# When p is turned and split in the last stage of an encoder layer, and when embedding weights may take raw slots

## The chip, the cores and the metric

One core of a Trainium2 chip runs the whole kernel. The metric is device microseconds of one launch, as a median over runs; lower is better.

## The reference, cut to what matters

N = 2048 tokens of width D = 1024 pass one encoder layer. What this change touches is the per-layer embedding, which the last layer norm takes in:

```python
x = layernorm(ALPHA * x0 + mix, ln1_g, ln1_b)              # x1 in the kernel
ffn = hierarchical_moe(x, ...)                             # two of 32 experts for each token
ple = sigmoid(x @ w_ple_gate + b_ple_gate) * (p @ w_ple_proj)   # 1024x1024 and 256x1024
out = layernorm(ALPHA * x + ffn + ple, ln2_g, ln2_b)
```

All products have to be of float32 accuracy.

## The kernel before, in words

A float32 product is made of three products of fp32r parts: every operand is split into a high part `hi` (a copy on ScalarE) and a low part `lo` (source minus `hi`, on VectorE). `split` (lines 304 and 305) does both, and `mm3` (lines 219 to 221) issues the three matmuls `hi*hi`, `hi*lo`, `lo*hi`. 128 tokens are a tile; there are 16.

**Places.** Buffers are slots of 4 KB per partition, handed out oldest-freed first. `SF` (tile `FB`, later also the region `FY`) holds split operands: 26 slots, and 12 more of `FY` during the mixer. `SR` (`RB`) holds raw rows and weights: 9 slots, and 12 more (`RY`) once `FY` has been given up. `SP` is the eight PSUM banks of 128x512; a pair of banks is two neighbours that begin at an even number, and of the free pairs the one whose later-freed bank has been free longest is taken. A taker that finds nothing free lets the other jobs go on until there is something. On the chip a buffer's next writer waits for its last reader.

**Order.** The program's text fixes which buffers every instruction gets. Running work (`run`) lets background jobs (`Background`, `start`, `need`) make a step after each `mm3`. A planner then orders the instructions of each engine by the times that it estimates, and each engine works through its own list in that order.

**Stages.** Mixer; output projection (`wo_tiles`), router and routing; the region passes from split to raw slots ("the region changes hands"); the embedding of tiles 10 to 15 (`PRE`, function `embed`); the 32 experts; the last stage.

**Weights.** From the last group of `wo_tiles` on, `load_weights` brings raw weights (line 1036, queue of SyncE) in the order: embedding for tiles 10 and 11, embedding for 12 to 15, experts, embedding for the last stage. It takes a raw slot only while more than `rkeep + rclaims` are free; `rkeep` is 3 and becomes 4 before the last stage. `split_weights` turns a raw weight into two split slots when two are free beyond `claims`. After the region's hand-over come `bp`, the broadcast bias of the gate (line 1296, issued by GpSimd), and the rows of p and x1 of tiles 10 and 11.

**Last stage.** For tiles 0 to 9 (`END`) one after the other, `embed_tile` takes a pair of banks, runs 48 matmuls for the gate (16 `mm3`), gives the tile's two slots of x1 back, adds the bias on VectorE (line 1231, once for each half of the columns), takes tanh on ScalarE (line 1232), runs 12 matmuls for the product with p, and combines (lines 1236, 1245). The 20 slots of embedding weights stay in place. `load_x1` brings x1's high and low parts of a tile, already split, into two slots (line 1145). `load_p` does the same for p of a pair of tiles: raw rows (line 1092), four transposes on TensorE into one bank (line 1125), one split slot, `split` with 512 columns each, and only then is the bank free:

```python
        b = SP.get()
        for k in range(4):
            nc.tensor.transpose(PS[:, b, k * 128:(k + 1) * 128], RB[:, r, k * 128:(k + 1) * 128], ident)
        SR.free(r)
        yield
        q, = yield from claimed(1)
        split(FB[:, q, :512], FB[:, q, 512:], PS[:, b])
        SP.free(b)
```

`release_p` frees p's slot after the second tile of its pair. `prepare_tile(i)` starts these jobs: for tile 0 while the last expert ends, for tile 1 just ahead of the loop, and for tile i + 2 after tile i. Called p0, p2, p4, p6, p8 are the p of tiles 0 and 1, 2 and 3, and so on.

Behind this runs `finish` for every tile: the gathered rows of the two experts (line 1616, GpSimd) are added with their weights (line 1653, VectorE), then mean, variance and the norm on GpSimd (1659, 1663 to 1665), ScalarE (1661, 1667), VectorE (1668) and VectorE or GpSimd (1669), and the output is stored (1672, issued by ScalarE).

Of the kernel before, what the change touches and what calls it, by code (L numbers as in the profile page):

```python
# [16 lines left out]
N = 2048  # L17
# [11 lines left out]
# Rows that the r-th fullest expert has a fixed place for; what goes beyond runs in a loop.  # L29
# [9 lines left out]
def most_further_blocks():  # L39
    """At least the most blocks beyond the fixed ones: counts fall with the rank, each is at most N, 2 N in all."""  # L40
    best = 0
    for m in range(1, NE + 1):
        need = [0] * m
        for r in range(m - 1, -1, -1):
            need[r] = max(CAPS[r] + 1, need[r + 1] if r + 1 < m else 0)
        left = 2 * N - sum(need)
        if left >= 0 and need[0] <= N:
            best = max(best, sum(-(-(need[r] - CAPS[r]) // 128) for r in range(m)) + left // 128 + m)
    return best
# [3 lines left out]
# first tiles, whose normalised rows are computed a second time for the residual  # L53
AGAIN = 8
# tiles at the end that take the rows of their experts before their embedding
# [3 lines left out]
def interleave(a, b):  # L59
    """The items of b spread evenly between those of a."""  # L60
    out = []
    for i, v in enumerate(a):
        out.append(v)
        out += b[i * len(b) // len(a):(i + 1) * len(b) // len(a)]
    return out
# [5 lines left out]
# tiles whose embedding comes before the experts, and after them  # L71
PRE, END = ([10, 11], [12, 13, 14, 15]), [0, 1, 2, 3, 4, 5, 6, 7, 8, 9]


class Slots:
    """A region cut into equal slots; the slot that has been free longest goes first."""

    def __init__(self, *parts):
        self.runs, n = [], 0
        for m in parts:  # L80
            self.runs.append((n, m))
            n += m
        self.age = {i: i - n for i in range(n)}
        self.clock = 0
        # slots from here on are only for those that ask for any; they take them first
        self.limit = 999
# [37 lines left out]
class Parts:  # L124
    """Slots of several tiles under one numbering."""
# [17 lines left out]
class Background:  # L143
    """Work that prepares what the tensor engine needs next, spread over the steps of the running work."""
# [36 lines left out]
def hybrid_conv_pool_hmoe_encoder(ctx, tc, x, p, ln0_g, ln0_b, w_in, b_in, conv_w, pool_w, pool_scale,  # L181
# [9 lines left out]
    # a region of the split tiles' at first, of the plain ones' later  # L191
# [34 lines left out]
    # constants  # L226
# [9 lines left out]
    # loads the table of functions while the first rows are on their way  # L236
# [34 lines left out]
    def start(name, gen, rate):  # L271
        jobs[name] = gen
        bg.add(gen, rate)

    def need(name):
        """Ends a job; the others go on when it has to wait for them."""
        if name in jobs:
            gen = jobs.pop(name)
            n = 0
            while next(gen, DONE) is not DONE:  # L280
                n += 1
                if n > 40:
                    bg.step()
            bg.forget(gen)

    # layer norm of a row tile in place
# [27 lines left out]
    # ---------------------------------------------------------------- mixer, first half  # L314
# [9 lines left out]
    def prep(c):  # L324
# [8 lines left out]
        for q in range(2):  # L333
# [15 lines left out]
            # gain and shift come after the transposes, where they are scalars of the partitions  # L349
# [31 lines left out]
    def again():  # L381
        """The rows of the first tiles, for which nothing is kept while the tensor engine waits for them."""
        gr0.append(SR.get())
        gr0.append(SR.get())
        nc.scalar.dma_start(RB[:, gr0[0]], bcast(ln0_g, D))
        nc.scalar.dma_start(RB[:, gr0[1]], bcast(ln0_b, D))
        for t in range(AGAIN):
            yield from wait(SR, keep=2)
            r = SR.get()
            nc.sync.dma_start(RB[:, r], xf[t * 128:(t + 1) * 128, :])  # L390
            yield
            v = RB[:, r]
            s = ln_stats(v)
            yield
            ln_apply(v, s, RB[:, gr0[0]], RB[:, gr0[1]])
            nc.gpsimd.dma_start(x0d[t * 128:(t + 1) * 128, :], v)
            SR.free(r)
            yield
# [21 lines left out]
    def load_w(s, j):  # L420
        """The four channel tiles h, gate_c, gate_b, u of group j."""
        for i in range(4):
            if (s, j, i) not in raw:
                yield from wait(SR)
                fetch_w(s, j, i)
                yield
            yield from wait(SF)
            hi = SF.get()
            yield from wait(SF)
            lo = SF.get()  # L430
            r = raw.pop((s, j, i))
            split(FB[:, hi], FB[:, lo], RB[:, r])
            SR.free(r)
            wz[s, j, i] = (hi, lo)
            yield
# [105 lines left out]
    # per-channel constants as columns: b_in, conv_w, pool_scale, ln0_g, ln0_b  # L541
# [9 lines left out]
    b = SP.get()  # L551
# [20 lines left out]
    def load_wo():  # L572
        """The output projection; its rows for the pools come times the pools' own products and scales."""
# [86 lines left out]
    # ---------------------------------------------------------------- mixer, second half; router  # L660
# [12 lines left out]
    # high parts next to low parts, and high parts alone  # L673
# [39 lines left out]
    def post(t, b, skip):  # L713
        """Residual, layer norm, x1 to memory and, transposed and split, to the chunk's tiles."""
# [70 lines left out]
    # ---------------------------------------------------------------- routing  # L785
# [33 lines left out]
    # by the rank of an expert: first row and rows of its whole blocks, rows of all its fixed places,  # L819
    # what a row's number beyond the whole blocks changes by, and the same beyond the fixed places  # L820
# [8 lines left out]
    def first_max(dst, val, best, n):  # L829
        """One-hot of the first place along the last axis where val equals best."""  # L830
# [5 lines left out]
    def expm(dst, tmp):  # L836
        """exp of values that are at most 0, from tanh of their halves."""
# [47 lines left out]
    def table(dst, val):  # L885
        """val[rank] by its slopes, ranks along the partitions."""
# [16 lines left out]
    def dispatch():  # L903
# [11 lines left out]
        # rank of every expert by its count, the lower number first among equals  # L915
# [21 lines left out]
        # further blocks, and how many come before every expert's  # L937
# [39 lines left out]
        # the token of every place: one-hot of the place in its block times the token's number at its block  # L977
# [30 lines left out]
    # ---------------------------------------------------------------- weights of experts and embedding, in their order  # L1008
# [32 lines left out]
    def split_weights():  # L1041
        while True:
# [6 lines left out]
            if kind == "P" and i % 5 == 4:  # L1049
                # half the product, for the sigmoid as (tanh + 1) / 2  # L1050
# [8 lines left out]
    # slots of the split tiles' that work under way is to get before further weights do  # L1059
    claims, rclaims = [0], [0]  # L1060
    rkeep, routed = [3], []
# [24 lines left out]
    # ---------------------------------------------------------------- per-layer embedding  # L1086
# [27 lines left out]
    def load_p(ts):  # L1114
        """The transposed parts of two tiles' rows of p, high and low halves in one slot."""
# [46 lines left out]
    def embed(ts, lhs, w, done, halves=(0, 1)):  # L1162
        """Gate times product and the residual, a half of the columns after the other."""
# [51 lines left out]
    def embed_tile(t, ws):  # L1215
        """The same for one tile, with all the weights at hand."""
# [36 lines left out]
    # ---------------------------------------------------------------- order of the work from here on  # L1253
# [34 lines left out]
    # the region changes hands  # L1288
# [5 lines left out]
    SR.add(NR, NY)  # L1294
    bp = SR.get()
# [53 lines left out]
    # every block: the tokens of its rows, its first row, whether it is half; the blocks of every expert  # L1349
# [46 lines left out]
    # ---------------------------------------------------------------- experts  # L1396
    def product(o, xs, k, wh, wl, start, stop):
        """Rows times weights. Half blocks hold high and low parts side by side: their products add up later."""
# [7 lines left out]
    def stage1(ns, w):  # L1406
        """Both products of the blocks ns with w1 and w3, every weight tile once."""
# [112 lines left out]
    # ---------------------------------------------------------------- rows beyond the fixed blocks  # L1520
# [48 lines left out]
    # ---------------------------------------------------------------- rows in the fixed blocks  # L1569
# [13 lines left out]
    def prepare_tile(i):  # L1583
        if i < len(END):
            t = END[i]
            if i % 2 == 0:
                claims[0] += 1
                start(f"p{t}", load_p(END[i:i + 2]), 1.0)
            claims[0] += 2
            start(f"x{t}", load_x1(t, True), 1.0)  # L1590

# [11 lines left out]
    # ---------------------------------------------------------------- combination and last layer norm  # L1603
    yq = {}

    def fetch(ts):
        """For every tile the rows of the two experts of its tokens, and what they are added to."""
# [13 lines left out]
    def finish_last(t):  # L1621
        """The rows of the experts before the embedding, which ends the work of the tensor engine."""
# [22 lines left out]
    def finish(t):  # L1645
# [12 lines left out]
        # mean from the sum, variance from the squares about it  # L1658
# [64 lines left out]
```

## Time and profile before

| what | value |
|---|---|
| median of three runs | 1624.23 us (1621.86 to 1624.94) |
| span of the profiled execution | 1625.7 us; no time of its own is given beside the span |
| TensorE busy | 1572.1 us, 97% of the span |
| VectorE, ScalarE, GpSimd busy | 71%, 49%, 29% |
| last matmul ends | 1610.4 us after the span's start |

The profiled execution's span lies 1.5 us above the median. TensorE is busy nearly throughout, so what counts are the few stretches in which it stands still or runs at a lower granted clock.

### The profile page before, as it was taken

What the parts mean: (1) busy time and instruction counts of PE and PEld (TensorE: products, weight loads), DVE (VectorE), ACT (ScalarE), POOL (GpSimd) and SP (SyncE); (2) the same over time, 40 slices, a digit from 0 to 9 for tenths busy, and PEclk for the clock granted to TensorE, in tenths of its full rate; (3) what the DMA queues carried; (4) which work ended last, traced back from release to release, by engine and by line L of the source; (5) the groups of instructions that cost most, each with busy time, mean ns of one, the idle gap of its engine ahead of it and who ended that gap; (6) DMA issues with size and microseconds to landing.
All of it is one profiled execution on the core that took longest, in us unless ns stands there. A gap on an engine that the chain in (4) does not pass through costs nothing.

```text
span 1625.7 us, 21580 instructions
## 1 busy us (share of the span) xinstructions
PE 1572.1 (97%) x7370; PEld 1293.2 (80%) x7371; DVE 1157.1 (71%) x1406; ACT 792.6 (49%) x940; POOL 476.4 (29%) x626
## 2 busy tenths in 40 slices
PE   6999999999999998999999999999999999999986
PEld 6887888887888887778888888888888888888865
DVE  6777484345666767758878788777888767776887
ACT  7343242113111124147777777677777657662332
POOL 3454152443232225010212111111212101006874
PEclk9999999999999999999999999999999999999988
DMA  6547268865375536469898998998898987998871
GB/s 207 183 154 222 65 186 293 299 248 165 116 264 196 178 120 240 141 217 381 310 381 322 359 352 303 355 357 333 324 360 313 347 275 268 369 338 327 325 272 65
DMA packets 204810, 427.88 MB, mean 263 GB/s; under 512 B 18857, under 2 KB 70617, under 8 KB 204697
## 3 DMA queue, kind: packets, MB, share of 16 engines
q1 hardware_dynamic: 162096, 292.33, 51.6%
q0 software_dynamic: 34080, 122.96, 20.4%
q10 hardware_dynamic: 8520, 11.18, 2.1%
q8 instruction: 59, 0.97, 0.2%
q14 instruction: 55, 0.44, 0.1%
HBM read 333.10 MB, written 93.32 MB: 262 GB/s over the span
## 4 chain that ended last, share of the span: by engine, by line
PE 37%; issue 11%; POOL 4%; DVE 1%; DMA 1%; ACT 1%; POOLq 0%; DVEq 0%; ACTq 0%; SPq 0%
PE PS L219 9%; PE PS L221 9%; PE PS L220 9%; PE PS L1403 3%; PE PS L1404 3%; PE PS L311 2%; POOL RY L1616 1%; PE PS L1461 1%; DMA yd<-RB 1%; DVE RB L1653 0%; POOL RY L1669 0%; POOL RB L1616 0%; POOL rstd L1664 0%; PE PS L1331 0%; POOL rstd L1663 0%
## 5 line engine op out<-in xcount | busy, mean ns | idle before, releaser
L220 PE MATMUL PS<-FB 128*128 128x512 f32 (+1 forms) x1516 | 590.2, 389 | 5.5 <-DVE FB L305 5.5
L219 PE MATMUL PS<-FB 128*128 128x512 f32 (+1 forms) x1436 | 560.0, 392 | 12.8 <-DVE FB L305 8.1
L221 PE MATMUL PS<-FB 128*128 128x512 f32 (+1 forms) x1436 | 558.4, 390 | 3.1 <-DVE FB L305 3.1
L220 PEld LDWEIGHTS PS<-FB 128*128 128x128 f32 x1516 | 287.9, 190 | 62.2 <-DVE FB L305 6.2
L219 PEld LDWEIGHTS PS<-FB 128*128 128x128 f32 x1436 | 272.7, 190 | 68.1 <-DVE FB L305 9.0
L221 PEld LDWEIGHTS PS<-FB 128*128 128x128 f32 x1436 | 272.4, 190 | 57.9 <-DVE FB L305 3.5
L305 DVE TENSOR_TENSOR FB<-RY,FB 128x1024 fp32r<-128x1024 f32 x232 | 280.8, 1229 | 52.1 <-ACT FB L304 25.7
L305 DVE TENSOR_TENSOR FB<-RB,FB 128x1024 fp32r<-128x1024 f32 x212 | 257.4, 1227 | 79.6 <-ACT FB L304 67.8
L304 ACT CAST FB<-RB 128x1024 fp32r<-128x1024 f32 x216 | 223.7, 1049 | 148.5 <-PE PS L220 50.1
L304 ACT CAST FB<-RY 128x1024 fp32r<-128x1024 f32 x236 | 243.6, 1051 | 92.9 <-PE PS L220 45.1
L1316 POOL DMA_INDIRECT RY<-x1d,TBI x29 | 56.5, 1948 | 391.8 <-DVE FB L305 217.2
L305 DVE TENSOR_TENSOR FB<-PS,FB 128x1024 fp32r<-128x1024 f32 (+1 forms) x116 | 103.1, 897 | 68.4 <-ACT FB L304 68.2
L304 ACT CAST FB<-PS 128x1024 fp32r<-128x1024 f32 (+1 forms) x116 | 86.4, 759 | 113.7 <-PE PS L311 75.6
L220 PE MATMUL PS<-FB,FY 128*128 128x512 f32 x264 | 104.4, 396 | 0.0
L1403 PE MATMUL PS<-FB 128*128 128x512 f32 x264 | 103.9, 394 | 0.0
L1404 PE MATMUL PS<-FB 128*128 128x512 f32 x264 | 103.2, 391 | 0.0
L219 PE MATMUL PS<-FB,FY 128*128 128x512 f32 x216 | 86.0, 398 | 0.0
L221 PE MATMUL PS<-FB,FY 128*128 128x512 f32 x216 | 85.6, 396 | 0.0
L219 PE MATMUL PS<-FY,FB 128*128 128x512 f32 x180 | 72.1, 400 | 0.0
L304 ACT CAST FY<-RB 128x1024 fp32r<-128x1024 f32 (+1 forms) x30 | 31.0, 1035 | 82.5 <-PE PS L220 56.5
L221 PE MATMUL PS<-FY,FB 128*128 128x512 f32 x180 | 71.0, 395 | 0.0
L296 POOL TENSOR_SCALAR rstd<-mv 128x1 f32<-128x1 f32 x42 | 29.4, 701 | 138.2 <-DVE mv L291 125.3
(275 smaller groups left out, 2006.5 us busy)
## 6 DMA issues: line engine op xcount, KB each, us to landing
RY<-in_w_dram SPq DMA_DIRECT2D x224, 512.0 KB, 9.2
RB<-in_w_dram SPq DMA_DIRECT2D x160, 512.0 KB, 8.7
yd<-RB POOLq DMA_DIRECT2D x59, 512.0 KB, 8.3
RB<-in_w_in_dram SPq DMA_DIRECT2D x32, 512.0 KB, 5.7
RB<-in_x_dram SPq DMA_DIRECT2D x24, 512.0 KB, 4.9
yd<-RY POOLq DMA_DIRECT2D x23, 512.0 KB, 7.0
x1Td<-FB POOLq DMA_DIRECT2D x20, 512.0 KB, 5.4
FB<-x1Td SPq DMA_DIRECT2D x20, 512.0 KB, 7.2
```

The source lines that it names most:

```text
L219: nc.tensor.matmul(o, ah, bh, start=start, stop=False)
L220: nc.tensor.matmul(o, ah, bl, start=False, stop=False)
L221: nc.tensor.matmul(o, al, bh, start=False, stop=stop)
L296: nc.gpsimd.tensor_scalar(rstd[:, s:s + 1], mv[:, s, 1:2], EPS, None, op0=OP.add)
L304: nc.scalar.copy(hi, src)
L305: eng.tensor_sub(lo, src, hi)
L311: nc.tensor.transpose(v[:, k], src[:, k * 128:(k + 1) * 128], ident)
L1316: nc.gpsimd.indirect_dma_start(out=RB[0:64 if half else 128, rows[n]], out_offset=None, in_=x1d, in_offset=bass.IndirectOffsetOnAxis(ap=id ...
L1403: nc.tensor.matmul(o, xs[0][:, c], wh, start=start, stop=False)
L1404: nc.tensor.matmul(o, xs[0][:, c], wl, start=False, stop=stop)
L1461: nc.tensor.transpose(v[:, k], g[:, k * 128:(k + 1) * 128], ident[0:m, 0:m])
L1616: nc.gpsimd.indirect_dma_start(out=RB[:, yq[t, i]], out_offset=None, in_=yd, in_offset=bass.IndirectOffsetOnAxis(ap=SLI[:, i, t:t + 1], ax ...
```

## The change

In the last stage p of a pair of tiles is started earlier. Before, `prepare_tile(i)` with even i started p of tiles i and i + 1, and then x1 of tile i. After, x1 comes first, and p of tiles i + 2 and i + 3 behind it: call 0 starts p0, call 1 p2, call 2 p4, call 4 p6, call 6 p8. Second, `rkeep` is 0 until the region has changed hands and 3 from then on. The rest of the diff removes comments and docstrings.

```diff
-    rkeep, routed = [3], []
+    rkeep, routed = [0], []
...
     RB.add(late.tile([128, NY, 1024], F32, name="RY"), NR, NY)
     SR.add(NR, NY)
+    rkeep[0] = 3
     bp = SR.get()
...
     def prepare_tile(i):
         if i < len(END):
             t = END[i]
-            if i % 2 == 0:
-                claims[0] += 1
-                start(f"p{t}", load_p(END[i:i + 2]), 1.0)
             claims[0] += 2
             start(f"x{t}", load_x1(t, True), 1.0)
+        for j in {0: (0,), 1: (2,)}.get(i, (i + 2,)):
+            if i % 2 == 0 or i == 1:
+                if j < len(END):
+                    claims[0] += 1
+                    start(f"p{END[j]}", load_p(END[j:j + 2]), 1.0)
```

## Rows read from the trace of the kernel before

**Rows 1.** The page's head and its busy times by engine.
```profile
span 1625.7 us, 21580 instructions
...
PE 1572.1 (97%) x7370; PEld 1293.2 (80%) x7371; DVE 1157.1 (71%) x1406; ACT 792.6 (49%) x940; POOL 476.4 (29%) x626
```

**Rows 2.** Waits of TensorE: total us, times, longest us.
```profile
PE PS L357 <- ACT RB L346: 13.1, 4, 8.9
PE PS L219 <- DVE FB L305: 8.1, 2, 7.8
PE PS L220 <- DVE FB L305: 5.5, 2, 4.3
PE PS L219 <- DVE ZB L1184: 3.5, 2, 2.9
```

**Rows 3.** Busy time by stretch of the last stage (tile 4, gap, tile 6, tail).
```profile
core 0: us, PE busy (x) PEld busy (x) DVE busy (x) ACT busy (x) POOL busy (x), PEclk, DMA share, GB/s
...
1517.30:1530.90 13.60, 13.60 (x62) 11.26 (x61) 12.69 (x15) 3.64 (x5) 11.36 (x9) 1.00 1.01 383
...
1545.30:1553.10 7.80, 0.03 (x1) 0.00 (x0) 7.02 (x9) 5.20 (x7) 7.41 (x9) 0.63 0.42 158
1553.10:1568.70 15.60, 15.58 (x60) 12.68 (x60) 10.56 (x9) 6.61 (x8) 14.84 (x14) 0.86 0.90 325
...
1610.40:1625.70 15.30, 0.03 (x1) 0.00 (x0) 6.89 (x11) 0.56 (x1) 1.71 (x2) 0.67 0.11 42
```

**Rows 4.** Timeline of TensorE in tile 5, at p6: start us, us.
```profile
1536.54 0.60 PE L1125 MATMUL PS<-ident,RY 128*128 128x128 f32 x4
```

**Rows 5.** Timeline of ScalarE around the copies of p2 and p6.
```profile
1470.99 0.59 ACT L304 CAST FB<-PS 128x512 fp32r<-128x512 f32 x1 [5.78 <-PE PS L221]
...
1546.40 1.24 ACT L1667 ACTIVATE RY<-RY,nbias,rstd 128x1024 f32<-128x1024 f32 x1 [5.25 <-POOL nbias L1665]
...
1551.04 0.56 ACT L304 CAST FB<-PS 128x512 fp32r<-128x512 f32 x1
```

**Rows 6.** Timeline of VectorE: bias adds, low parts of p, one multiply.
```profile
1475.75 1.37 DVE L1231 TENSOR_TENSOR ZB<-PS,RB 128x512 f32<-128x512 f32 x2 [10.60 <-PE PS L221]
1477.04 0.68 DVE L305 TENSOR_TENSOR FB<-PS,FB 128x512 fp32r<-128x512 f32 x1
...
1517.21 0.68 DVE L305 TENSOR_TENSOR FB<-PS,FB 128x512 fp32r<-128x512 f32 x1
...
1521.42 1.28 DVE L1231 TENSOR_TENSOR ZB<-PS,RB 128x512 f32<-128x512 f32 x2
...
1536.85 1.23 DVE L1668 TENSOR_TENSOR RB<-RB,RY 128x1024 f32<-128x1024 f32 x1 [1.36 <-ACT RB L1667]
...
1552.38 0.69 DVE L305 TENSOR_TENSOR FB<-PS,FB 128x512 fp32r<-128x512 f32 x1
1556.97 3.42 DVE L1668 TENSOR_TENSOR RB<-RB,RY 128x1024 f32<-128x1024 f32 x1 [3.90 <-ACT RB L1667]
1560.31 1.27 DVE L1231 TENSOR_TENSOR ZB<-PS,RB 128x512 f32<-128x512 f32 x2
```

**Rows 7.** Timeline of GpSimd beside VectorE's multiply of 1556.97.
```profile
1556.91 2.39 POOL L1669 TENSOR_TENSOR RY<-RY,RB 128x1024 f32<-128x1024 f32 x1
```

**Rows 8.** Timeline of SyncE's queue around the hand-over of the region.
```profile
596.86 1.24 SPq L1036 DMA_DIRECT2D RB<-in_w_ple_gate_dram  x2
602.90 0.37 SPq L1092 DMA_DIRECT2D RB<-in_p_dram  x1
605.38 0.34 SPq L1097 DMA_DIRECT2D RY<-x1d  x1
...
617.37 5.41 SPq L1036 DMA_DIRECT2D RB<-in_w_ple_gate_dram  x3
```

**Rows 9.** Busy time by stretch, from the hand-over to the next gap.
```profile
605.40:634.00 28.60, 28.57 (x146) 23.25 (x144) 19.80 (x24) 13.70 (x15) 14.69 (x11) 1.00 0.96 348
```

**Rows 10.** Timeline of ScalarE ahead of TensorE's gap at 634.
```profile
630.31 1.05 ACT L304 CAST FB<-RB 128x1024 fp32r<-128x1024 f32 x1 [4.59 <-DMA RB<-in_w_ple_gate_dram]
```

**Rows 11.** Bias add of tiles 10 to 15: count, ns, first and last start.
```profile
L1184 DVE TENSOR_TENSOR ZB<-PS,RB x5: 677/684/691, 616.1 to 653.8; 128x512 f32<-128x512 f32 x5
```

## The prediction, on record before the changed kernel ran

> **What bounds the kernel now.** I began with the page's head: TensorE is busy 1572.1 us of a span of 1625.7 [rows 1], so no engine has to become faster; what can be won or lost is TensorE's idle time and stretches at its lower clock. The waits of TensorE say where the idle time is [rows 2]. The largest entry is the kernel's start (L357), which the diff doesn't touch. Then come one wait of 7.8 us and one of 4.3 us for the low part of a split (DVE L305), and one of 2.9 us for the bias add of the earlier embedding (L1184). The stretches of the last stage place the 7.8 us between tiles 5 and 6, from 1545.3 to 1553.1 [rows 3]; the 4.3 us and the 2.9 us lie at 634 and 652, in the embedding of tiles 10 to 15. So both edits have a gap in their reach.
>
> **Why tile 6 waits.** p6 is turned at 1536.54 [rows 4] into one bank, which stays taken until VectorE has made p6's low part, from 1552.38 to 1553.07 [rows 6]; TensorE goes on at 1553.1. I followed the rule of the bank pairs through the last stage by hand: p6's bank is 6, and tile 6 is given banks 6 and 7. So tile 6 waits because its bank still holds p6, not because it needs p6 itself. The copy was late since ScalarE stood still for 5.25 us ahead of 1546.40, waiting for GpSimd's part of an older tile's norm, and had four operations between that and p6's copy at 1551.04 [rows 5]. The gap costs more than its 7.8 us: tile 6 takes 15.6 us at a mean granted clock of 0.86, where tile 4 takes 13.6 at 1.00 [rows 3], so 2.0 more go to matmuls at the lower of the two levels (1.2 instead of 2.4 GHz).
>
> **Edit 1, p two pairs ahead: instructions.** It adds and removes none: four transposes (0.60 us) [rows 4], a copy (0.56 us) [rows 5] and a subtraction (0.69 us) [rows 6] for each pair remain. x1's loads come ahead of p's in SyncE's queue, p's rows come one pair earlier, and x1 of a tile is issued one tile or more ahead of use as before: I take these at zero, since a tile of 13.6 us [rows 3] covers even a load of 12.9 us, from 617.37 [rows 8] to 630.31 [rows 10]; without that cover one tile would wait up to those 12.9.
>
> **Edit 1: slots.** What changes is the place that p gets. Of the 26 split slots 20 hold weights, x1 of two tiles takes 4, and two pairs of p take 2: now all 26 are in use. p2 gets the last one at once. p4, p6 and p8, started behind x1 of tiles 2, 4 and 6, find none, until tile 1, 3 or 5 has ended its gate matmuls and gives its two slots back. But the transposes come ahead of the claim on a slot. So p is turned early, into a bank, and then stands there until the running tile's gate is over. "Split two pairs ahead" is for these three "turned early, bank held". Carrying the bank rule on under this order, I get: p4 holds bank 3 from tile 1 on, which no tile uses before tile 3, long after; p6 holds bank 1 through tile 3, and tile 4 is given banks 0 and 1; p8 holds bank 6 through tile 5, and tile 6 is given 6 and 7, as before.
>
> **Edit 1: when VectorE reads the bank.** The slot comes free with the end of the gate, which is also what the bias add L1231 of that tile waits for. Before, only p2 was in this position: its copy ran at 1470.99 [rows 5], and its low part at 1477.04, straight behind both bias adds of tile 0, which began at 1475.75 [rows 6]. I take this order for p6 and p8 too.
>
> - Tile 4: the bias adds of tile 3 begin at 1521.42 and end 1.28 later, p6's low part would run from 1522.7 to 1523.4. Tile 4 begins at 1517.3 and needs its second bank (the low column half goes first, three matmuls of some 0.23 us) at 1518.0. Gap: 5.4 us, perhaps with 2 us of lower clock. Before, p4's low part was over at 1517.89 [rows 6] and there was none.
> - Tile 5 then ends at 1545.3 + 5.4 = 1550.7, or at up to 1552.7.
> - Tile 6: VectorE is behind by then. The bias adds of tile 5 began only at 1560.31 [rows 6], because VectorE stood still for 3.90 us for the norm of another tile and then spent 3.42 us on one multiply; this chain through GpSimd and ScalarE doesn't depend on TensorE, so I leave it where it is. p8's low part: 1560.31 + 1.27 + 0.69 = 1562.27, against 1553.07 for the low part that tile 6 waited for before. Tile 6 starts 9.2 us later. What tile 4 lost is contained in that, since the end of tile 5 is no longer what tile 6 waits for. The lower clock behind the gap stays at 2.0 us, as before.
> - All that follows, tiles 6 to 9 and the tail of 15.3 us [rows 3], moves along. Edit 1: **+9.2 us**.
>
> Bounds of this term: if the low part stands behind the first bias add only, 0.6 less. If the multiply takes 1.23 us, as at 1536.85, and not 3.42 [rows 6], 2.2 less. If ScalarE's copy is put behind the tanh of the same tile, 1 to 3 us more. So +6.4 to +12.
>
> The multiply took 3.42 us while GpSimd ran an addition of 2.39 us that began 0.06 us earlier [rows 7]. The Trainium skill, "SBUF — State Buffer", section "SBUF: two separate sides", says that VectorE with two inputs and GpSimd exclude each other for a whole instruction on a shared pair of ports; 1.23 + 2.39 = 3.62 is near the 3.42, so the trace agrees here. By that rule the multiply stays slow only as long as the two still meet, which is the 2.2 us of the second bound.
>
> **Edit 2, rkeep 0 until the hand-over.** Before, the nine old raw slots were filled late: the last two gate weights went in at 596.86, `bp` before that, p's rows at 602.90; the rest went into the new region from 605.38 on [rows 8]. Without the reserve the loader takes all free slots: I count two further gate weights (512 KB each) loaded before 605. But `bp` (512 KB) and p's rows (256 KB) then find no old slot and go into the region, not before 605.4. In the stretch from 605.4 to 634.0 the DMA engines are busy at 0.96 and move 348 GB/s [rows 9]: the net 0.25 MB less is worth 0.25 MB / 348 GB/s = 0.7 us. The gap at 634 follows from ScalarE's wait of 4.59 us for a weight that was issued in a group from 617.37 [rows 8] and arrived at 630.31 [rows 10]; if all comes 0.7 us earlier, the gap of 4.3 us shrinks by that. I take **-0.7 us**. Bounds: with the whole 1 MB counted, 2.9 us of the gap and 2 us of lower clock, -5; with the gaps at 634 and 652 gone, -9.2 (4.3 + 2.9 + 2.0, the last by the loss at tile 6). On the other side `bp` is first read at 616.1 [rows 11], 10.7 us after 605.4; a load of 12.9 us as above would make it 2.2 us late, and p's rows some 1 us: +3. The experts behind it have loads of their own and no gap, so no other stage gives this back.
>
> **Sum.** 1625.7 + 9.2 - 0.7 = 1634.2 for the span. Runs lie 1.5 us below the profiled span in the median: **1632.7 us**.
>
> **The rivals.**
>
> 1. *Faster.* p6 and p8 are split early after all: the planner sets their copy and low part ahead of the bias adds, or VectorE isn't behind. For it: work is handed out earlier in the text, and VectorE is only 71% busy [rows 1]. Against it: the slot isn't free before the gate's end. Then tile 6 starts at 1545.3 and ends at 1558.9. Tile 7's banks are tile 5's, read by the bias adds of 1560.31 to 1561.58 [rows 6]; it starts at about 1561.3 instead of 1568.7: -7.4. 1625.7 - 7.4 - 0.7 - 1.5 = 1616.1 us. It decides if p8's bank is free before about 1546; at 1553 nothing is won. The Trainium skill, "Perfetto Trace Analysis", section "Optimization Strategy", says to make what a gap waits for start sooner, which is this rival; the same section says that bubbles on the engine that should be saturated can mean too little SBUF or PSUM for the next tile, which is my forecast. The trace bears out the second more, since the bank, not p, is late. Chance 0.20.
> 2. *No change.* p8's low part lands where p6's did, ahead of the bias adds at about 1552.4, and tile 4 sees no wait as before: only edit 2 is left, 1623.5. For it: VectorE had a free place there, since it idled 3.90 us. Chance 0.14.
> 3. *Edit 2 pays back edit 1.* Both gaps at 634 and 652 close: 1625.7 + 9.2 - 9.2 - 1.5 = 1624.2. Against it: half of the loads saved comes back as `bp` and p. Chance 0.09.
> 4. *Slower still.* `bp` and p's rows stall TensorE by 3 us at 610 to 616: 1632.7 + 0.7 + 3 = 1636.4. Chance 0.07.
>
> **How the numbers follow.** My forecast has 0.50, with a range of its own of 1628 to 1637 (6.4 to 12 for edit 1, -2 to 0 for edit 2). About 0.2%, 3.2 us, is what a measurement can tell from no change: 1621.0 to 1627.5. Below it lie rival 1 and a part of rivals 2 and 3: 0.24; inside most of these two: 0.20; above it my forecast and rival 4: 0.56. The range goes from rival 1's middle, 1616, to 1637; beyond it remain half of rival 1 and the upper ends, some 0.17.
>
> **What would show it.** Transposes L1125 of p6 in tile 3 and of p8 in tile 5; a new gap of about 5 us inside the first matmuls of tile 4, and one ahead of tile 6 that ends some 9 us later than 1553, both put down to DVE L305; low parts of 128x512 straight behind bias adds L1231. For edit 2: two more gate weights into RB before 605, and the gap at 634 smaller by about 0.7. I am wrong if the low parts of p6 and p8 run ahead of those bias adds, if the chain through GpSimd puts the bias adds of tile 5 elsewhere than 1560, or if the gaps at 634 and 652 change by more than 3 us.

## The result, and the profile after

The changed kernel took 1633.26 us in the median of six runs (1629.86 to 1634.64), against 1624.47 us for the kernel before in six: a ratio of 1.0055, interval 1.0044 to 1.0066. It is slower by 8.8 us; 1632.7 had been forecast. The profiled execution took 1634.11 us, with a span of 1632.5, which is 6.8 us longer than the span of before [rows 1]. These are two single executions; why their difference is smaller than that of the medians is taken up with the prediction below.

The page's head and the busy times of the changed kernel:

```profile
span 1632.5 us, 21571 instructions
...
PE 1573.1 (96%) x7371; PEld 1293.3 (79%) x7371; DVE 1159.3 (71%) x1406; ACT 792.1 (49%) x940; POOL 475.7 (29%) x626
```

No engine has more than 2.2 us more to do. The waits of TensorE in the changed kernel (total us, times, longest us), to be held against [rows 2]:

```profile
...
PE PS L219 <- DVE FB L305: 11.0, 3, 5.9
PE PS L219 <- DVE ZB L1184: 3.5, 2, 2.9
PE PS L1125 <- DMA RY<-in_p_dram: 2.9, 1, 2.9
PE PS L220 <- DVE FB L305: 2.4, 2, 1.3
```

Two waits for low parts (5.9 and 4.7 us) stand where one of 7.8 was; the 4.3 us wait of L220 at 634 is down to 1.1; the transposes of p of tiles 10 and 11 wait 2.9 us for their rows, which is new. By stretch of the last stage (columns as in [rows 3]):

```profile
core 0: us, PE busy (x) PEld busy (x) DVE busy (x) ACT busy (x) POOL busy (x), PEclk, DMA share, GB/s
...
1520.00:1526.00 6.00, 0.07 (x2) 0.06 (x1) 6.00 (x6) 0.63 (x1) 5.23 (x4) 0.69 0.81 305
...
1557.40:1562.10 4.70, 0.05 (x1) 0.00 (x0) 3.34 (x5) 2.34 (x3) 4.70 (x4) 0.76 1.01 408
1562.10:1576.00 13.90, 13.87 (x52) 11.29 (x53) 10.32 (x11) 5.61 (x9) 10.28 (x9) 0.84 0.78 260
...
1613.90:1632.50 18.60, 0.02 (x1) 0.00 (x0) 9.59 (x16) 1.23 (x2) 2.20 (x3) 0.61 0.15 56
```

The gaps are in tile 4 (1520 to 1526) and in tile 6 (to 1562.1), and the tail behind TensorE's last matmul is 18.6 us instead of 15.3. TensorE turns p6 in tile 3 and p8 in tile 5:

```profile
1507.58 0.60 PE L1125 MATMUL PS<-ident,RB 128*128 128x128 f32 x4
...
1545.47 0.60 PE L1125 MATMUL PS<-ident,RB 128*128 128x128 f32 x4
...
1557.06 0.39 PE L220 MATMUL PS<-FB 128*128 128x512 f32 x1
1562.13 0.79 PE L219 MATMUL PS<-FB 128*128 128x512 f32 x1 [4.68 <-DVE FB L305]
```

And VectorE, with the two low parts of 512 columns (L305) and the bias adds (L1231) of tiles 3, 5 and 9. Line 1672 is the multiply that is line 1668 before; lines behind `prepare_tile` have moved down by four:

```profile
1524.61 0.68 DVE L1231 TENSOR_TENSOR ZB<-PS,RY 128x512 f32<-128x512 f32 x1
1525.21 0.68 DVE L305 TENSOR_TENSOR FB<-PS,FB 128x512 fp32r<-128x512 f32 x1
1525.81 0.68 DVE L1231 TENSOR_TENSOR ZB<-PS,RY 128x512 f32<-128x512 f32 x1
...
1558.80 2.08 DVE L1672 TENSOR_TENSOR RB<-RB,RY 128x1024 f32<-128x1024 f32 x1 [1.36 <-ACT RB L1671]
1560.80 0.68 DVE L1231 TENSOR_TENSOR ZB<-PS,RY 128x512 f32<-128x512 f32 x1
1561.40 0.68 DVE L305 TENSOR_TENSOR FB<-PS,FB 128x512 fp32r<-128x512 f32 x1
...
1615.76 1.28 DVE L1231 TENSOR_TENSOR ZB<-PS,RY 128x512 f32<-128x512 f32 x2
```

What the reader is to see: p6 is turned at 1507.6, but its low part comes 17.6 us later, between the two bias adds of tile 3; p8 likewise, 15.9 us after it was turned, between those of tile 5. ScalarE's copies of p6 and p8 lie in between:

```profile
1517.72 0.56 ACT L304 CAST FB<-PS 128x512 fp32r<-128x512 f32 x1
...
1556.09 0.57 ACT L304 CAST FB<-PS 128x512 fp32r<-128x512 f32 x1
```

The copies ended 6.9 and 4.7 us before the low parts began. So at the end it was neither the slot nor the copy that the low part waited for, but its place in VectorE's list. Ahead of tile 4 that list was simply full: VectorE had no idle time from 1516.71 to the low part at 1525.21. One of the instructions in between, a weighted addition, took 3.36 us beside an addition of GpSimd:

```profile
1520.13 3.36 DVE L1657 SCALAR_TENSOR_TENSOR RB<-RY,GW,RB 128x1024 f32<-128x1024 f32 x1
...
1519.17 3.24 POOL L1673 TENSOR_TENSOR RB<-RB 128x1024 f32<-128x1024 f32 x1 [1.81 <-DVE RB L1672]
```

Ahead of tile 6 the list waited, 1.35 and 1.36 us for ScalarE's part of two norms, and then spent 2.08 us on a multiply.

### The profile page after: what moved, and what is told of

It reads as the page before. It is cut to its first block, busy times and chain, and to the rows that moved or that the text cites. A ratio compares the mean times of both kernels' runs of the same rounds, so it can differ in the third digit from the quotient of the medians.

```text
span 1632.5 us, 21571 instructions
## 1 busy us (share of the span) xinstructions
PE 1573.1 (96%) x7371; PEld 1293.3 (79%) x7371; DVE 1159.3 (71%) x1406; ACT 792.1 (49%) x940; POOL 475.7 (29%) x626
## 5 line engine op out<-in xcount | busy, mean ns | idle before, releaser
L220 PE MATMUL PS<-FB 128*128 128x512 f32 (+1 forms) x1516 | 590.2, 389 | 2.4 <-DVE FB L305 2.4
L305 DVE TENSOR_TENSOR FB<-RB,FB 128x1024 fp32r<-128x1024 f32 x234 | 285.6, 1235 | 83.7 <-ACT FB L304 66.3
L220 PEld LDWEIGHTS PS<-FB 128*128 128x128 f32 x1516 | 287.9, 190 | 59.3 <-DVE FB L305 3.4
L304 ACT CAST FB<-RB 128x1024 fp32r<-128x1024 f32 x238 | 246.8, 1050 | 157.7 <-PE PS L220 52.7
L305 DVE TENSOR_TENSOR FB<-RY,FB 128x1024 fp32r<-128x1024 f32 x210 | 253.8, 1225 | 43.4 <-ACT FB L304 22.2
L304 ACT CAST FB<-RY 128x1024 fp32r<-128x1024 f32 x214 | 221.2, 1051 | 79.4 <-PE PS L220 32.8
L305 DVE TENSOR_TENSOR FB<-PS,FB 128x1024 fp32r<-128x1024 f32 (+1 forms) x116 | 103.2, 899 | 64.4 <-ACT FB L304 62.8
L220 PE MATMUL PS<-FB,FY 128*128 128x512 f32 x264 | 104.4, 396 | 0.0
```

What stands on the lines that cost most here:

```text
L220: nc.tensor.matmul(o, ah, bl, start=False, stop=False)
L304: nc.scalar.copy(hi, src)
L305: eng.tensor_sub(lo, src, hi)
```

## The experiments

**One edit at a time.** e1 takes the line of edit 2 alone into the kernel before, e2 the new `prepare_tile` alone.

```diff
# e1                                   # e2
+    rkeep, routed = [0], []           (prepare_tile of the changed kernel,
+    rkeep[0] = 3                       rkeep stays 3)
```

> The kernel before with edit 2 alone (rkeep 0 until the hand-over). Theory (edit 1 costs all of it): within 1 us of the kernel before, that is 1623.5 to 1625.5, with p's rows and bp arriving late at about 608 (some 2 to 3 us of wait at the transposes of p of tiles 10 and 11) and the gap at 634 shortened by as much. Rival (edit 2 costs part of it): 1627 or more, that is at least 3 us slower than before.

> The kernel before with edit 1 alone (p two pairs ahead, x1 first). Theory: all of the loss is here, 1632 to 1634, with a gap in tile 4 that ends near 1526 and one in tile 6 that ends near 1562. Rival (edit 2 costs part of it): 1630 or less.

e1: 1624.99 us against 1624.38, ratio 1.0005, interval 0.9995 to 1.0014. e2: 1630.92 us, ratio 1.0040 (1.0027 to 1.0054). Edit 2 changes nothing that can be measured; the loss is edit 1's, 6.5 us, between the two expectations (1632 or more, 1630 or less); whether the two edits add something together is within the intervals. In the profile of e1 the transposes of p wait 2.6 us and the wait at 634 is 1.1 us, as expected. In the profile of e2 the gaps end at 1522.79 and 1558.99, some 3 us earlier than expected; 2.4 of these are that its last stage begins earlier than in the changed kernel (first matmul at 1453.0 against 1455.4).

**Is it the bank?** If tile 6 waits only because its pair contains the bank of p, another bank must help. In e3 and e4 the text gives p's bank back 24 steps later, so that the pairs of tiles 4 and 6 avoid it; the work and its readers stay.

```diff
         split(FB[:, q, :512], FB[:, q, 512:], PS[:, b])
-        SP.free(b)
         for i, t in enumerate(ts):
             pT[t] = (q, 2 * i)
+        for _ in range(24 if ts[0] in END else 0):
+            yield
+        SP.free(b)
```

> The changed kernel, but the text gives p's bank back 24 steps after the split instead of at once, so the bank pairs of tiles 4 and 6 no longer contain the bank that holds p6 or p8 (6 and 7 with p6 in bank 2, and 2 and 3 with p8 in bank 1). Nothing is taken away from the work, and p's low parts are as late as before. Theory (the tile waits for the bank, not for p): the gaps in tiles 4 and 6 go away, tile 7 then waits for the bias adds of tile 5 at about 1561, total 1614 to 1622. Rival (VectorE is the limit, the bank is only where it shows): the waits move to the bias adds or to the next pair and the time stays within 3 us of the changed kernel, 1630 or more.

> The kernel before, with the same later return of p's bank: p6 in bank 2, tile 6 in banks 6 and 7. Theory (bank): the gap of 7.8 us ahead of tile 6 and the lower clock behind it go, tile 7 waits for the bias adds of tile 5 until about 1561, total 1615 to 1620. Rival (VectorE is the limit): 1622 or more.

e3: 1637.78 us, ratio 1.0082 (1.0067 to 1.0096), slower than the changed kernel. e4: 1630.02 us, 1.0030 (1.0018 to 1.0043), slower than the kernel before. The theory that it is this bank alone has fallen. The waits of TensorE, first in e3, then in e4 (line 1233 is the bias add there, 1238 the combining, two lines down):

```profile
PE PS L219 <- DVE ZB L1233: 7.2, 2, 6.5
PE PS L219 <- DVE ZB L1238: 6.5, 3, 4.9
```

```profile
PE PS L219 <- DVE ZB L1238: 12.0, 2, 8.7
```

The waits for L305 in the last stage are gone, and waits of 6.5, 4.9 and 8.7 us for other readers on VectorE have come: whichever bank the next tile got, its last reader stood in the same late list. The edit doesn't add a bank: it keeps one of the eight back for longer, so the tiles have fewer to go round, and part of the new waits can come from that. What a further free bank would do isn't shown. The Trainium skill, "Perfetto Trace Analysis", section "Optimizing Tensor Performance", has matmul groups rotate through the banks so that the reading of one overlaps the matmuls of the next; here the rotation was changed and the reader not, and the overlap didn't come.

**A slot at once.** e5 gives the last stage a 27th split slot (cut off the region after the hand-over, which keeps 11 raw slots), so that a turned p needn't wait for the gate's end.

```diff
-    RB.add(late.tile([128, NY, 1024], F32, name="RY"), NR, NY)
-    SR.add(NR, NY)
+    RB.add(late.tile([128, NY - 1, 1024], F32, name="RY"), NR, NY - 1)
+    SR.add(NR, NY - 1)
+    FB.add(late.tile([128, 1, 1024], F32R, name="FX"), 100, 1)
...
+    SF.add(100, 1)
     start_fetch(END[:6])
```

> The changed kernel with one more split slot for the last stage (the region after the hand-over has 11 raw slots instead of 12), so that p4, p6 and p8 find a slot as soon as they are turned and don't wait for the running tile's gate. The first prediction's mechanism (the bank stands until the gate's end because no slot is free): the low parts of p6 and p8 run in the middle of tiles 3 and 5, the waits on DVE L305 in tiles 4 and 6 go, 1616 to 1622. Rival (VectorE's lateness is the limit, whatever the bank holds): the waits on L305 go, but waits for the bias adds or the combining (L1231, L1236) of tiles 4 and 5 take their place, VectorE comes to tile 5's bias adds at about 1560 again, and the time is between 1623 and 1633.

e5: 1638.11 us, ratio 1.0079 (1.0065 to 1.0094). Both expected times were missed. The waits came as the rival had them: none of note for L305 in the last stage, but 4.6 us for the combining (L1236) and 2.6 us for p6's copy in tile 4. The rows of p6 were loaded 20 us later than in the changed kernel (1510.6 against 1490.3, with one raw slot fewer), it was turned at 1522.56, and even then, with a slot at hand, its copy came 12.7 us later. ScalarE's timeline in e5:

```profile
1534.12 1.15 ACT L1667 ACTIVATE RB<-RB,nbias 128x1024 f32<-128x1024 f32 x1 [5.80 <-POOL nbias L1665]
...
1535.27 0.56 ACT L304 CAST FB<-PS 128x512 fp32r<-128x512 f32 x1
```

So a free slot doesn't bring the split: ScalarE stood at a step of another tile's norm that waited for GpSimd. As a test of the slot alone e5 isn't clean, since the loads moved too.

**Norms in the lists.** e6 and e7 take the last addition of a norm, 2.4 us of GpSimd's time, to VectorE for three tiles of four (eleven additions in all), in the kernel before and in the changed one; e8 spreads the norms over more of the stage.

```diff
-        (nc.gpsimd if t % 4 else nc.vector).tensor_add(a, a, RB[:, b2])
+        nc.vector.tensor_add(a, a, RB[:, b2])
# e8 alone
-    start("y", fetch(tail), 0.2)
+    start("y", fetch(tail), 0.17)
```

> The kernel before with the last addition of the norm in the last stage on VectorE for all tiles, instead of on GpSimd for three of four. GpSimd loses 2.4 us for each of these tiles, VectorE gains 1.2 us and no longer meets GpSimd there. Theory (VectorE comes late to tile 5's bias adds because it waits in line for a norm whose small steps stand in GpSimd's queue): the bias adds of tile 5 come 4 us or more earlier than 1560, the gap ahead of tile 6 shrinks by at least 4 us, 1612 to 1621. Rival (VectorE is simply full in these tiles): bias adds later by some us, 1624 or more.

> The changed kernel with the same edit. Theory (GpSimd's queue): it comes down by as much as the kernel before or more, to 1615 to 1625. Rival (VectorE is full): 1632 or more.

> The kernel before with the fetching of rows for the last norm spread over more of the last stage (rate 0.17 instead of 0.2 for each step), so that fewer norms stand in VectorE's list in tiles 2 to 5 and more in tiles 7 to 9. Theory (the norms of other tiles, which TensorE doesn't need, make VectorE late for what TensorE needs): the bias adds of tiles 4 and 5 lag less (by 3 us or more), the gap ahead of tile 6 shrinks, 1614 to 1622. Rival (the order at tile 6 is what counts, not the load): the gap stays within 1 us, 1623 or more.

e6: 1623.19 us, ratio 0.9991 (0.9980 to 1.0001), neither theory's number: the gap ahead of tile 6 is 6.55 us, only 1.2 less. e7: 1621.56 us, ratio 0.9982 (0.9969 to 0.9994) to the kernel before, 11.7 us below the changed kernel's median, as the theory had it; with VectorE full it would have stayed at 1632 or more. e8: 1636.86 us, 1.0073 (1.0060 to 1.0086), against the theory and as the rival had it: the gap stays at 8.1 us and the last bias adds come at 1619.63.

The changed kernel and e7 in one stretch each, from the last stage's first tile to the end of TensorE's work, first the changed kernel:

```profile
1456.00:1614.00 158.00, 147.31 (x639) 120.58 (x638) 117.06 (x131) 52.31 (x70) 101.28 (x102) 0.96 0.73 264
```

```profile
1456.00:1606.00 150.00, 145.90 (x640) 119.55 (x640) 118.33 (x148) 53.80 (x74) 72.91 (x92) 0.99 0.76 282
```

VectorE is busy for as long (118.3 against 117.1 us), in 8 us less, though it has taken over eleven additions of 1.2 us; GpSimd has 73 instead of 101. The additions cost VectorE hardly anything because others became shorter. In this stretch of the changed kernel nine entries of VectorE's timeline ran beside an addition L1673 of GpSimd and took some 14 us more in all than the same work elsewhere in the stage; e7 has none of these. One group of weighted additions, first in the changed kernel, then in e7 (count, busy us, mean ns):

```profile
L1657 DVE SCALAR_TENSOR_TENSOR RB<-RB,GW 128x1024 f32<-128x1024 f32 x6 | 11.5, 1914 | 0.1
```

```profile
L1657 DVE SCALAR_TENSOR_TENSOR RB<-RB,GW 128x1024 f32<-128x1024 f32 x6 | 7.7, 1281 | 0.1
```

So e7 changes two things at once, GpSimd's list, whose small steps VectorE and ScalarE wait for, and the lengthened instructions, and it doesn't tell which brought the gain. The second alone isn't enough: the kernel before has as much of it in its last stage and e6 has none, yet e6 gains only 1.2 us, with zero inside its interval. TensorE's longest wait in the last stage of e7 is 3.4 us.

**Fewer norms.** e9 (kernel before) and e10 (changed kernel) leave out the additions and norms of tiles 10 to 15; their rows are still fetched and a base row is stored in place of the result.

```diff
     def finish(t):
         for _ in range(6):
             yield
+        if t not in END:
+            for i in range(2):
+                SR.free(yq.pop((t, i)))
+                yield
...
+            nc.scalar.dma_start(outf[t * 128:(t + 1) * 128, :], RB[:, base[t]])
+            SR.free(base.pop(t))
+            return
```

> The kernel before, leaving out the additions and norms of tiles 10 to 15 in the last stage (their rows are still fetched, and a base row is stored in place of the result): VectorE, ScalarE and GpSimd lose six norms, TensorE loses nothing. Theory (VectorE is late because norms stand in its list ahead of what TensorE waits for): no wait over 1 us in tiles 2 to 9, 1608 to 1615. Rival (the late low part of p comes from the place of its copy in ScalarE's list or its slot, whatever the load): the gap ahead of tile 6 stays at 4 us or more, 1617 or more.

> The changed kernel, leaving out the same six norms. Theory (held banks hurt only because VectorE is late): waits of at most 2 us in tiles 4 and 6, and a time within 3 us of the kernel before with the same left out. Rival (turning p ahead of its slot costs by itself): waits of 4 us or more remain in tiles 4 and 6, and it is 5 us or more slower than the kernel before with the same left out.

e9: 1627.24 us, ratio 1.0028 (1.0015 to 1.0042): slower than the kernel before with less to do. e10: 1620.79 us, 0.9971 (0.9955 to 0.9987): with the same left out, p two pairs ahead is now 6.5 us *faster*, where at most 3 us of difference had been expected. In e10 TensorE has no wait in tiles 0 to 9 that counts:

```profile
1456.00:1599.00 143.00, 143.00 (x638) 117.88 (x637) 85.88 (x102) 38.09 (x52) 62.70 (x71) 1.00 0.75 291
```

although the low parts of p6 and p8 come as late as in the changed kernel, between the two bias adds (VectorE of e10, at p6; line 1681 is the multiply of a norm):

```profile
1519.01 0.69 DVE L1231 TENSOR_TENSOR ZB<-PS,RY 128x512 f32<-128x512 f32 x1 [4.18 <-PE PS L221]
1520.94 1.23 DVE L1681 TENSOR_TENSOR RY<-RY 128x1024 f32<-128x1024 f32 x1 [1.24 <-ACT RY L1680]
1522.09 0.68 DVE L305 TENSOR_TENSOR FB<-PS,FB 128x512 fp32r<-128x512 f32 x1
```

Here VectorE waits for TensorE (4.18 us), not the other way round, and the bank that p6 holds costs nothing. The program gives p6, p8 and all tiles the same banks as in the changed kernel, and p6 and p8 hold theirs for longer: 20.2 and 21.1 us from the turning (1502.61 and 1530.38) to the end of the low part, against 18.3 and 16.6. So turning p ahead of its slot does not cost by itself. In e9 the theory missed its time, and so did the rival its gap: ahead of tile 6 no wait is longer than 1.7 us, but TensorE waits 6.0 us in tile 3 for p4's copy. VectorE and then ScalarE of e9 show why (line 1662 adds a gathered row, 1670 is the square of a norm):

```profile
1511.34 1.28 DVE L1662 SCALAR_TENSOR_TENSOR RY<-RY,GW 128x1024 f32<-128x1024 f32 x1 [7.90 <-DMA RY<-yd,SLI]
```

```profile
1513.79 1.15 ACT L1670 ACTIVATE RY<-RY,nbias 128x1024 f32<-128x1024 f32 x1 [9.69 <-POOL nbias L1668]
...
1514.94 0.56 ACT L304 CAST FB<-PS 128x512 fp32r<-128x512 f32 x1
```

With six norms fewer the next tile's stands further ahead in VectorE's list, and its gathered row hasn't landed: VectorE waits 7.9 us, ScalarE 9.7 us behind it, and the copy of p4 stands right behind. Less load, and a like stall.

**p6 and p8 alone.** e11 leaves p2 and p4 ahead and starts p6 and p8 when the kernel before does, but behind x1; e12 adds the edit of e7.

```diff
-        for j in {0: (0,), 1: (2,)}.get(i, (i + 2,)):
+        for j in {0: (0,), 1: (2,), 2: (4,), 4: ()}.get(i, (i,)):
```

> The changed kernel with p2 and p4 ahead as it has them, and p6 and p8 started in tiles 5 and 7 as before (behind x1). Theory (p6 and p8, turned into a bank that the next tile but none of its slots is free for, make the loss): no wait on L305 in tile 4, the gap ahead of tile 6 ends near 1553 again, 1621 to 1628. Rival (p2 and p4, or the order of x1 and p in the queues, make it): 1630 or more.

> The same as the last one, with the last addition of the norms on VectorE for all tiles. If the two effects add up (p6 and p8 back: about 8 us off the changed kernel; the addition moved: 1 us off the kernel before, 12 off the changed one): 1613 to 1623, the fastest so far. If the gain of the moved addition was only the changed kernel's own waits: 1623 to 1627.

e11: 1636.38 us, ratio 1.0078 (1.0056 to 1.0099): the loss is not undone, the theory missed and the rival's bound holds: the early start of p6 and p8 is not all of it. No profile of e11 is read here; by its program p6 still holds a bank of tile 6's pair, and p8 one of tile 8's, as in the kernel before. e12: 1626.25 us, 1.0017 (1.0001 to 1.0033), 4.7 us above e7 and within the second expectation: the two effects don't add up. In e12 TensorE waits 6.9 us in tile 6 for p6's copy; ScalarE there:

```profile
1558.70 1.15 ACT L1665 ACTIVATE RB<-RY,nbias 128x1024 f32<-128x1024 f32 x1 [9.11 <-POOL nbias L1663]
...
1560.89 0.56 ACT L304 CAST FB<-PS 128x512 fp32r<-128x512 f32 x1
```

Again a copy stands behind a norm's step, which had waited 9.1 us. Why p6 itself was turned only at 1552.6 there was not tried further.

## Why the prediction was right, and where its steps were not

- **Edit 2, -0.7 us: this step failed.** Two more gate weights were loaded before 605, as forecast, and the wait at 634 shrank from 4.3 to 1.1 us, by more than the 3 us that the prediction had named as a sign of being wrong; the granted clock in the 8 us behind it is 1.00 instead of 0.73. But p's rows, in the new region, made the transposes wait 2.9 us, the stall of rival 4, and rival 3's gain came at 634 alone. Behind the wait near 652, which stayed, the first matmuls now ran at the lower clock: the granted clock is 0.78 as a mean of the 7.8 us up to the next transposes, where the kernel before took 6.2 us at 1.00. The restart of TensorE, the transposes and this stretch (columns as in [rows 3]), first of the kernel before, then of the changed one:

```profile
654.52 0.50 PE L219 MATMUL PS<-FB 128*128 128x512 f32 x1 [2.85 <-DVE ZB L1184]
...
660.73 0.63 PE L1125 MATMUL PS<-ident,RB 128*128 128x128 f32 x4
...
654.50:660.70 6.20, 6.11 (x36) 4.66 (x38) 3.11 (x22) 0.84 (x2) 0.00 (x0) 1.00 0.79 284
```

```profile
651.87 0.80 PE L219 MATMUL PS<-FB 128*128 128x512 f32 x1 [2.87 <-DVE ZB L1184]
...
659.64 0.63 PE L1125 MATMUL PS<-ident,RB 128*128 128x128 f32 x4
...
651.80:659.60 7.80, 7.73 (x37) 5.84 (x38) 3.16 (x23) 0.84 (x2) 0.00 (x0) 0.78 0.63 240
```

  In the mixer, which the diff doesn't touch, the changed kernel's profiled execution was 2.0 us ahead (the same 1783 matmuls by 399.2 us against 401.2), at the restart near 652 it was 2.65 ahead, at the transposes behind it 1.1, and 1.1 still at the first transposes of the last stage (1453.68 against 1454.81). So edit 2 lost 0.9 us there instead of gaining 0.7. e1 measures +0.6 us, with zero inside its interval.
- **Edit 1, slots and banks: as forecast.** p6 and p8 are turned in tiles 3 and 5, and their low parts run only among the bias adds of these tiles; tiles 4 and 6 wait for L305. By the program p6 has bank 1 and tile 4 banks 0 and 1, as forecast; p8 has bank 4 and tile 6 banks 4 and 5 where 6 and 6 and 7 had been forecast, with the same effect. The low parts came behind the first of the two bias adds (the bound with 0.6 less).
- **Tile 4's gap: the size by two errors.** 5.9 us were measured and 5.4 forecast. The low part ended at 1525.89 instead of 1523.4, 2.5 us later, and TensorE stopped at 1520.0 instead of 1518.0, because it had more of the other column half to do first.
- **The place of tile 5's bias adds: near the forecast.** 1560.80, against 1560.31 before [rows 6]; p8's low part at 1561.40 to 1562.08 against 1562.27 forecast for its end; TensorE went on at 1562.13, 9.0 us later than before. But the changed kernel had entered the last stage 1.1 us earlier, so measured from there the bias adds come 1.6 us later and not where they were, and TensorE's restart 10.1 us later, where the sum had 9.2. The way there was another too: two waits of 1.35 and 1.36 us and a multiply of 2.08, in place of 3.90 and 3.42 us.
- **"All that follows moves along": this step failed.** It took tile 6 to stand still from its first matmul. A held bank stops one column half only, and the planner had put matmuls of the other half ahead: TensorE ran until 1557.45 and had done 22 matmuls of tile 6. From the restart to the end the kernel before had 244 matmuls to do, the changed one 218; four of the difference of 26 are p8's transposes, the others these 22 (the first row is of the kernel before, the second of the changed one):

```profile
1553.10:1610.50 57.40, 57.31 (x244) 46.80 (x244) 48.46 (x55) 20.10 (x27) 36.52 (x34) 0.96 0.56 202
```

```profile
1562.10:1614.00 51.90, 51.78 (x218) 42.36 (x218) 40.78 (x46) 15.34 (x22) 26.15 (x26) 0.96 0.43 152
```

  That gives 5.5 us back: TensorE's end moved by 3.5 us only. The other 3.3 us are the longer tail, which the prediction held fixed at 15.3. The last tile's bias adds ran at 1615.76 against 1609.02, 6.7 us later, while TensorE was done 3.5 us later: VectorE had not caught up. In every profile read here, before, after and eleven experiments, the span ends 16.7 to 17.5 us after the last tile's first bias add. This is the row that sets the end, and the prediction didn't have it.
- **The sum: right by luck.** Counted from the mixer on, the changed kernel's span is 6.8 + 2.0 = 8.8 us longer, which is what the medians differ by. This is made of 10.1 for the restart, 5.5 back, 3.3 for the tail and 0.9 for edit 2; the forecast had 9.2 and -0.7, together 8.5. Errors of +0.9, -5.5, +3.3 and +1.6 leave +0.3. That the kernel gets slower, and through which waits, was forecast for the right reason; that the time was met within 0.6 us was not.
- **The cause behind the bank.** The prediction named the held bank as the reason and VectorE's lateness as the size. e10 shows that the same early turning, with the same banks held for longer, is harmless when VectorE isn't behind. e3 and e4 show that tiles with other banks wait for other late readers in VectorE's list, and lose as much or more. e5, e9 and e12 show a like stall on ScalarE, each time a copy behind a step of a norm that waits for GpSimd, in e9 because a gathered row hadn't landed. How much of VectorE's lateness is such waiting, and how much the instructions that last longer beside GpSimd's additions, was not separated.
- **Rival 1** (1616 us) needed p8's bank free before 1546; no experiment brought that about together with the full work.

Open: which of its two effects makes e7 faster; why e11 is as slow as the changed kernel, and how much of each result is the planner's new order, since every edit reorders all the lists; e8's loss was not traced either.

The fastest version with all the work in it is e7, the changed kernel with the last addition on VectorE: 0.18% below the kernel before, by an interval that ends just short of none.

## What to carry to other kernels

Starting work earlier in the program moves nothing on an engine that works through a list in order, as long as a step ahead of it in that list is late: look at what stands ahead in the list, what that waits for and what it takes beside another engine's work, not at the engine's busy share. Before preparing an operand further ahead, count the places it needs at each step (here a bank before a slot): taken in the wrong order, the early start only holds a scarcer place for longer, which costs as soon as the place's last reader is late. And if the end of the kernel always follows one instruction by the same time, forecast that instruction, not the busiest engine's last.

## What the runs showed that was not expected

- Leaving out six norms made the kernel slower (e9, +0.28%) or faster (e10, -0.29%), depending on which of the two kernels they were left out of.
- GpSimd at 101 us of 158 busy was never the busiest engine of the stage, yet taking 28 us off it (e7) shortened the changed kernel by 11.7 us, and the kernel before by 1.2 us, which is within its interval.
